# The S5 operator matrices moved from the middle of a diffusion layer to its beginning, beside the context's first feed-forward

## The chip, the cores and the metric

The kernel runs on one core of a Trainium2 chip, as one launch. The metric is the device time of that launch in microseconds, the median of three runs. The core has five engines with in-order queues: TensorE (PE: matmul, and PEld for its weight loads), VectorE (DVE), ScalarE (ACT), GpSimd (POOL) and SyncE (SP). In this kernel every DMA is issued from the SP queue, and a DMA that has to wait there holds back all that stand behind it.

## The reference, cut to what matters

```python
x   = half_ffn(x, mod_x, 0, ...)      # latents, 512 tokens, SwiGLU, width 1024, hidden 2816
ctx = half_ffn(ctx, mod_c, 0, ...)    # context, 256 tokens, same weights
hc  = modulate(ctx, norm_g[l, 1], mod_c[3], mod_c[4])
hx  = modulate(x, norm_g[l, 1], mod_x[3], mod_x[4])
out_c, ctx_states = token_mixers(hc, 1, zero_states(...), p, need_ctx)   # only the states are used
out_x, _ = token_mixers(hx, rows, ctx_states, p, True)
x = x + mod_x[5] * out_x
x = half_ffn(x, mod_x, 2, ...)
return rmsnorm(x, final_g)

def token_mixers(h, ...):             # S5 scan beside RWKV-7 scan, each in both directions
    proj = h @ w_in
    dt = exp(log_dt); mag = exp(dt * lam_re)
    ab = mag * (cos(dt * lam_im) + 1j * sin(dt * lam_im))
    z = (ab - 1) / lam; bb = z * b     # S5: 32 groups, 64 states, 16 channels each
    s5: s = ab * s + bb @ u; y = real(c @ s)
    rwkv: S = S * w + (S @ aa) bb^T + v k^T; y = S @ r      # 8 heads of 64
    ...
```

Neither the S5 matrices (powers of `ab`, `z`, and products of them with `b` and `c`) nor their inputs depend on the tokens: they can be made at any time before the first S5 scan.

## The kernel before, in words

The program is written by generators ("streams") that a planner class `Plan` runs in turn. Each stream has a priority number and yields what it needs next: a tile, an event by name, or a pair such as `("V", 600)`, which asks that the planned backlog of VectorE is at most 600 ns. `Plan.run` takes the stream with the lowest number whose needs are met at the planned time of TensorE, and the instructions are put into the engines' queues in that order. The planner's order is fixed when the program is built; on the chip only the queues and the semaphores count. A recording layer issues every instruction, so in the profile nearly all of them have the line L209, and tiles tell them apart.

**The dense work** is a stream of priority 9 (`dn`). It walks a list of weight tiles of 128 output columns: SP loads `raw` (512 KB), ACT casts it to the high half `wh`, DVE or POOL subtracts to make the low half `wl`, and PE takes three matmuls for each 128x128 tile (`hx,wh`, `hx,wl` and a second `wh` with the low half of the input; `ah`/`al` are the hidden activations in the down products). The list holds the context's first FFN (C, 256 columns, tiles `hc`, output `c`), the latents' first FFN (X, 512 columns, `hx`, output `x`), and from its eighth item on, among the latter, the context's input projections (`win`).

**The start.** `mods01` (priority 1) makes the first eight modulation pieces: two loads of `wmod` (512 KB each, four buffers), eight PE matmuls on each, an ACT copy to `mrow`, two PE matmuls `sel,mrow` into bank 6, and a DVE addition `mod<-b,bmod`. Bank 6 is a single buffer, so a `sel` matmul waits for the DVE addition before it. `norm0` sums the context's squares (`accc`), and after it the first FFN matmul (`hc,wh`) runs. `bg_a` makes the other modulations during the context's FFN and posts `wm`.

**`s5_build`** makes the S5 matrices. Its prelude is 85 small DVE operations in three parts (two exponentials and the sine's argument, 38, and 6 behind the two ACT sines; the powers `pw` and the factor `z`, 35; their products `pz`, 6). Then 16 blocks follow, each of 6 POOL operations (four `ms`, two `X`), 4 DVE copies (`cb`), 4 PE transposes (`ident,X`), 4 PE matmuls (`cb,X`), two ACT copies (`gst`, `kst`) and 6 DMAs (`hb`, `hk` in, `GTd`, `Kd` out). A second stream `outputs` has 16 blocks of 4 DVE `mh`, 2 DVE `H`, and DMAs (`hc` in, `Hd` out). At the end `Kd` is read back and turned into `KTd` (15 DMAs) and `KTe` (8 DMAs), and the event `s5b` is posted.

**The context's mixer** is laid out by `ctx_run` (priority 3). After the context's norm it opens the pool of the S5 matrices, adds `s5_build`, and then the projections. The scan stage waits for `s5b` among others:

```python
yield ["s5b", "winc"] + [f"{n}c{j}" for n in ("pb", "vr") for j in range(4)]
```

That stage loads `AB`, `Z`, `AT` (the products of the RWKV part, stored before as `abk`, `vt`, `lf`), `U` and `gt` for S5, solves a triangular system on DVE (`prod<-Tl,AT` and `Tl<-Tl,prod`, 62 operations), sends the solution through DRAM (`ti`, `tt`, `T`), and then runs four chunks on PE (`T,M`, `tt,w`, `ident,AB`, `Z,M`, `R,tt`, ...). What is left of the latents' FFN (`X`, dense) fills gaps of this stage; its last part waits for an event posted after the scan. The latents' mixer later has the same steps.

Of the kernel before, what the change touches and what calls it, by code (L numbers as in the profile page):

```python
# [27 lines left out]
MFB = 2  # L28
SPD = 0
WOL = 4  # L30
S5V = 600
S5Q = 3000
MPV = 1200
SPLIT_AT = 0
S5P = 3
FILLP = 5
RECP = 0
GATE0 = 0
# [245 lines left out]
class Kern:  # L284
# [575 lines left out]
    def phase_a(self):  # L860
        nc, a, sch, X, C = self.nc, self.a, self.sch, self.X, self.C
        with ExitStack() as es:
            self.hid = {}
            self.wxs, self.wx = self.right("wx")
            self.w_slots(self.wx, 1, 0, self.n_gate)
            self.hcs, hcp = self.right("hcp")
            C.h = [hcp.tile([128, KT, NCT], F32R, name=f"hc{i}") for i in range(2)]
            wrs, self.wxr = self.right("wxr")
            self.w_slots(self.wxr, 0, 1)
            self.cas, C.fp = self.right("ca")  # L870
            C.fp2 = C.fp
            C.res = C.fp.tile([128, KT, NCT], F32, name="c1")
            C.acc = [[C.fp.tile([128, 256], F32, name=f"accc{i}") for i in range(2)]]
            sch.post("fp0c")
            wms, self.wm = self.right("wm")
            st = [sch.add(self.mods01(), 1), sch.add(self.norm0(C), 0)]
            sch.add(self.dn, 9)
            sch.run(*st)
            nxs, self.nx = self.right("nx")
            X.res = es.enter_context(self.pool("rp")).tile([128, KT, NX], F32, name="x1")  # L880
            sch.add(self.bg_a(wms, nxs), 4)
            sch.add(self.norm0(X), 5)
            self.ctxg = sch.add(self.ctx_run(es, wrs), 3)

            def body(b, c, k, pb):
                return self.modulated(X.fp2, X.res[:, k, c], pb, 1, k, 0, [t[:, k, c] for t in X.h])

            def last():
                yield ["rwc"]
                yield from self.norm(X.fp2, X, 0, body)  # L890

            sch.run(sch.add(last(), 1))
            sch.run(sch.add(self.w_retire(self.wy), 0))
            self.wys.close()
# [13 lines left out]
    def ctx_run(self, es, wrs):  # L908

        X, C, sch = self.X, self.C, self.sch  # L910
        yield ["wm", "dl0c0", "hx17"]
        X.fp = es.enter_context(self.pool("fpx"))
        sch.post("fp0x")
        self.dbanks = (0, 5, 2)

        def body(b, c, k, pb):
            return self.modulated(C.fp, C.res[:, k], pb, 1, k, 1, [t[:, k] for t in C.h])

        yield from self.norm(C.fp, C, 0, body)
        self.cas.close()  # L920
        yield from self.w_retire(self.wxr)
        wrs.close()
        self.sbs, sb = self.right("sb")
        sch.add(self.s5_build(sb), S5P)
        qs, C.q = self.right("qc")
        self.phase_b1(C)
        for p, g in self.b1_gens:
            sch.add(g(C), p)
        yield ["s5b", "winc"] + [f"{n}c{j}" for n in ("pb", "vr") for j in range(4)]
        qs.close()  # L930
        self.sbs.close()
        self.hcs.close()
        rws, C.rw = self.right("rwc")
        self.rw_setup(C.rw)
        s5s, C.sp = self.right("s5c")
        C.hs = C.sp.tile([128, 32, 2, 32], F32, name="hs")
        self.dbanks = (0, 5)
        for p, g in ((0, self.rw_main(C)), (1, self.rw_pre(C)), (1, self.rw_solve(0, C.rw)), (2, self.s5_rec(C)),
                     (3, self.s5_in(C))):
            sch.add(g, p)  # L940
        yield ["step3", "s5recc"]
        s5s.close()
        rws.close()
        self.wms, wm = self.right("wm2")
        self.fill = sch.add(self.fill_run(wm), FILLP)
        X.fp2 = es.enter_context(self.pool("fpx2"))
        X.acc = [[X.fp2.tile([128, 256], F32, name=f"accx{b}{i}") for i in range(2)] for b in range(2)]
        self.wys, self.wy = self.right("wy")
        self.w_slots(self.wy, 2, 0, self.n_win)
        self.dbanks = (0, 5, 1)  # L950
        sch.post("rwc")
        sch.post("fp0x2")


    def s5_build(self, sb):
# [109 lines left out]
        def outputs():  # L1065

            nxt = load(0, "hc", a["s5C"])
            for n, (d, h2) in enumerate(todo):
                (Ct, c), nxt = nxt, load(n + 1, "hc", a["s5C"]) if n < 15 else None
                yield [Ct, ("V", S5V)]  # L1070
                H, ms = half("H"), half("mh")
# [11 lines left out]
                                      H[:, r].rearrange("p (e f) -> p e f", e=2))  # L1083
            self.sch.post("s5h")

        self.sch.add(outputs(), S5P)
        nb, nx = load(0, "hb", a["s5B"]), load(0, "hk", a["s5C"])
        for n, (d, h2) in enumerate(todo):
            (B, c), (Ct, c) = nb, nx
            if n < 15:  # L1090
                nb, nx = load(n + 1, "hb", a["s5B"]), load(n + 1, "hk", a["s5C"])
            yield [B, ("P", S5Q)]
            ks = slice(7, None, -1) if d == 0 else slice(0, 8)
            X, ms = half("X"), half("ms")
            for o, (r0, b0, r1, b1, op) in enumerate(terms):
                Pg.tensor_mul(r4(ms[:, 0]), bk(pz, r0, ks, c), bb(B[:, b0]))
                Pg.tensor_mul(r4(ms[:, 1]), bk(pz, r1, ks, c), bb(B[:, b1]))
                Pg.tensor_tensor(X[:, o], ms[:, 0], ms[:, 1], op=op)
            yield [X, Ct, ("A", 1500)]
            for q in range(2):  # L1100
                p = slice(q * 64, (q + 1) * 64)
                V.tensor_copy(cb[p, 0, :, q * 16:(q + 1) * 16], Ct[p, 0])
                V.tensor_scalar(cb[p, 1, :, q * 16:(q + 1) * 16], Ct[p, 1], -1.0, None, op0=OP.mult)
            pb = self.bank(7)
            xe = lambda r, e: X[:, r, e * 128:(e + 1) * 128]
            for e in range(2):
                for r in range(2):
                    PE.transpose(pb[:, (2 * e + r) * 128:(2 * e + r + 1) * 128], xe(r, e), self.ident)
            st = sb.tile([128, 2, 256], F32, name="gst", bufs=1)
            A_.copy(st, pb.rearrange("p (e f) -> p e f", e=2))  # L1110
            nc.sync.dma_start(self.GTd[2 * h2:2 * h2 + 2, :, d].rearrange("e p f -> p e f"), st)
            yield [cb]
            pk = self.bank(6)
            for e in range(2):
                o = pk[:, e * 32:(e + 1) * 32]
                PE.matmul(o, xe(0, e), cb[:, 0, e], start=True, stop=False)
                PE.matmul(o, xe(1, e), cb[:, 1, e], start=False, stop=True)
            ks = sb.tile([128, 64], F32, name="kst")
            A_.copy(ks, pk[:, 0:64])
            nc.sync.dma_start(Kd[d, :, h2 * 64:(h2 + 1) * 64], ks)  # L1120
        yield ["s5h"]

# [1016 lines left out]
```

## Time and profile before

| | |
|---|---|
| three runs | 1898.08, 1900.58 and 1901.99 us, median 1900.58 |
| the profiled execution | 1891.72 us, span 1890.0 us, granted PE clock 0.939 of full |
| busy in the span | PE 1672.3 us (88%), DVE 996.4 (53%), ACT 716.9 (38%), POOL 687.5 (36%) |
| chain that ended last | PE 56%, DVE 14%, DMA 14%, ACT 6%, POOL 3%, SP queue 3% |

All views are of the profiled execution. Busy time is what an engine's instructions took; idle time of an engine that nothing waits for costs nothing. PE is the engine with the most work, so a stretch is read by how much of it PE was idle or had a clock below 1.00, and by what ended its idle time.

The stages by time: the modulations and loads to about 97 us, the context's FFN to 277.5, the context's projections among the latents' FFN to 690, the context's scan to 805.6, then the rest of the latents' FFN, the latents' mixer and the second FFN.

### The profile page before, as it was taken

The numbers are of one execution on the slowest core, as the hardware profiler recorded it, in microseconds if no ns is written. First come the engines' busy times: TensorE is split into PE (matmuls) and PEld (weight loads), VectorE is DVE, ScalarE is ACT, GpSimd is POOL, SyncE is SP. The second block draws the span as 40 slices with busy tenths as digits, with TensorE's granted clock in tenths as the row PEclk, the third lists the DMA queues.
The fourth block names the chain that finished last, engine by engine and source line by source line (L and its number), as shares of the span: only waits on it lengthen the run. The fifth ranks groups of instructions, "written<-read, shape, count | busy, mean of one in ns | idle before, by whom it ended". The sixth has DMA issues, their size and how long they took to land.

```text
span 1890.0 us, 33157 instructions
## 1 busy us (share of the span) xinstructions
PE 1672.3 (88%) x13208; PEld 1400.3 (74%) x13208; DVE 996.4 (53%) x1747; ACT 716.9 (38%) x1200; POOL 687.5 (36%) x815
## 2 busy tenths in 40 slices
PE   6889999999999988778976789968697999999996
PEld 3689987778878867665544567758587988888886
DVE  3376564755558728355788855643343433333335
ACT  3355442545463212535443333443443332222222
POOL 0144231555764314621334537660065421111111
PEclk9999999999999999888988889979799999999998
DMA  9955541335454474433753566466364223323231
GB/s 310 331 167 195 183 155 57 113 106 159 143 160 140 141 190 151 119 123 128 252 160 105 148 223 188 118 172 176 123 215 159 67 69 101 99 91 101 98 101 56
DMA packets 235626, 278.43 MB, mean 147 GB/s; under 512 B 93616, under 2 KB 186800, under 8 KB 234448
## 3 DMA queue, kind: packets, MB, share of 16 engines
q1 hardware_dynamic: 235472, 276.32, 47.8%
q8 instruction: 104, 1.70, 0.4%
q14 instruction: 50, 0.41, 0.1%
HBM read 234.31 MB, written 43.22 MB: 147 GB/s over the span
## 4 chain that ended last, share of the span: by engine, by line
PE 56%; DVE 14%; DMA 14%; ACT 6%; issue 4%; POOL 3%; SPq 3%; DVEq 0%; ACTq 0%; POOLq 0%
PE b L209 56%; DMA wmod<-in_wmod 3%; SPq L209 3%; POOL wl L209 2%; ACT wh L209 2%; DMA Hd<-H 2%; DMA raw<-in_wgu 2%; DVE st L209 1%; DVE mh L209 1%; DVE wl L209 1%; DMA gt<-gates 1%; DVE rs L209 1%; DVE prod L209 1%; DVE cvr L209 1%; DVE H L209 1%
## 5 line engine op out<-in xcount | busy, mean ns | idle before, releaser
L209 PE MATMUL b<-hx,wh 128*128 128x512 f32 (+1 forms) x2432 | 698.2, 374 | 22.6 <-ACT wh L209 10.9
L209 POOL TENSOR_TENSOR wl<-raw,wh 128x1024 fp32r<-128x1024 f32 x135 | 329.3, 2443 | 822.0 <-ACT wh L209 748.1
L209 PEld LDWEIGHTS b<-hx,wh 128*128 128x128 f32 x2432 | 439.1, 194 | 106.7 <-issue 19.0
L209 PE MATMUL b<-hx,wl 128*128 128x512 f32 (+1 forms) x1216 | 448.6, 369 | 7.6 <-POOL wl L209 6.0
L209 ACT CAST wh<-raw 128x1024 fp32r<-128x1024 f32 x273 | 283.1, 1046 | 196.3 <-DMA raw<-in_wgu 69.8
L209 DVE TENSOR_TENSOR wl<-raw,wh 128x1024 fp32r<-128x1024 f32 x138 | 187.3, 1358 | 276.9 <-ACT wh L209 274.5
L209 PEld LDWEIGHTS b<-hx,wl 128*128 128x128 f32 x1216 | 235.7, 194 | 47.9 <-POOL wl L209 8.6
L209 PE MATMUL b<-ah,wh 128*128 128x512 f32 (+1 forms) x560 | 196.8, 351 | 3.6 <-ACT wh L209 2.0
L209 PE MATMUL b<-ah,wl 128*128 128x512 f32 (+1 forms) x560 | 194.9, 348 | 1.9 <-POOL wl L209 1.9
L209 PE MATMUL b<-al,wh 128*128 128x512 f32 (+1 forms) x560 | 194.7, 348 | 0.0
L209 PE MATMUL b<-hc,wh 128*128 128x256 f32 x928 | 173.1, 287 | 1.2 <-ACT hc L209 1.2
L209 PEld LDWEIGHTS b<-hc,wh 128*128 128x128 f32 x928 | 145.8, 192 | 10.9 <-issue 8.2
L209 PE MATMUL b<-hc,wl 128*128 128x256 f32 x464 | 131.7, 284 | 0.0
L209 PEld LDWEIGHTS b<-ah,wh 128*128 128x128 f32 x560 | 108.0, 193 | 16.6 <-ACT wh L209 2.2
L209 PEld LDWEIGHTS b<-ah,wl 128*128 128x128 f32 x560 | 107.9, 193 | 15.2 <-POOL wl L209 2.1
L209 ACT CAST ah<-prod 128x512 fp32r<-128x512 f32 (+1 forms) x68 | 36.6, 538 | 212.6 <-DVE prod L209 212.5
L209 PEld LDWEIGHTS b<-al,wh 128*128 128x128 f32 x560 | 107.8, 192 | 12.1
L209 ACT ACTIVATE sil<-b 128x512 f32<-128x512 f32 (+1 forms) x68 | 35.0, 515 | 149.8 <-PE b L209 149.6
L209 PEld LDWEIGHTS b<-hc,wl 128*128 128x128 f32 x464 | 89.3, 192 | 0.0
L209 DVE TENSOR_TENSOR prod<-sil,b 128x512 f32<-128x512 f32 (+1 forms) x68 | 39.6, 582 | 93.0 <-PE b L209 74.4
L209 DVE SCALAR_TENSOR_TENSOR x1c<-b,gp,x1c 128x512 f32<-128x512 f32 (+1 forms) x67 | 43.9, 662 | 81.2 <-PE b L209 81.2
L209 PE MATMUL b<-wmod,zs 128*32 128x256 f32 x576 | 54.3, 465 | 19.3 <-DMA wmod<-in_wmod 19.1
(289 smaller groups left out, 2331.0 us busy)
## 6 DMA issues: line engine op xcount, KB each, us to landing
raw<-in_wgu SPq DMA_DIRECT2D x132, 512.0 KB, 3.9
wmod<-in_wmod SPq DMA_DIRECT2D x72, 512.0 KB, 5.3
raw<-in_wdn SPq DMA_DIRECT2D x66, 512.0 KB, 3.7
raw<-in_win SPq DMA_DIRECT2D x49, 512.0 KB, 4.0
gt<-GTd SPq DMA_DIRECT2D x32, 256.0 KB, 3.8
abk<-st SPq DMA_DIRECT2D x8, 1024.0 KB, 5.5
AB<-abk SPq DMA_DIRECT2D x8, 1024.0 KB, 6.3
GTd<-gst SPq DMA_DIRECT2D x16, 256.0 KB, 2.4
```

The lines of the kernel that those rows point to most:

```text
L209: r = f(out, *args, **kw)
```

## The change

The pool `sb` is opened in `phase_a`, under the buffers of the context's FFN, and the stream `s5_build` is added there, before the planner has run anything, with priority 6. The pool of the latents' FFN (`fpx`) is opened only after the context's norm is done and the context's FFN pool (`ca`) is closed. Inside `s5_build`, the 16 blocks and `outputs` wait for `wm`, the transposes use bank 4 in place of bank 7, the two DMAs out wait in the plan for their copies, and the allowed planned backlogs become 250 ns for DVE and 600 ns for POOL.

```diff
--- before.py
+++ after.py
@@ -28,11 +28,11 @@
 MFB = 2
 SPD = 0
 WOL = 4
-S5V = 600
-S5Q = 3000
+S5V = 250
+S5Q = 600
 MPV = 1200
 SPLIT_AT = 0
-S5P = 3
+S5P = 6
 FILLP = 5
 RECP = 0
 GATE0 = 0
@@ -865,6 +865,7 @@
             self.w_slots(self.wx, 1, 0, self.n_gate)
             self.hcs, hcp = self.right("hcp")
             C.h = [hcp.tile([128, KT, NCT], F32R, name=f"hc{i}") for i in range(2)]
+            self.sbs, sb = self.right("sb")
             wrs, self.wxr = self.right("wxr")
             self.w_slots(self.wxr, 0, 1)
             self.cas, C.fp = self.right("ca")
@@ -875,6 +876,7 @@
             wms, self.wm = self.right("wm")
             st = [sch.add(self.mods01(), 1), sch.add(self.norm0(C), 0)]
             sch.add(self.dn, 9)
+            sch.add(self.s5_build(sb), S5P)
             sch.run(*st)
             nxs, self.nx = self.right("nx")
             X.res = es.enter_context(self.pool("rp")).tile([128, KT, NX], F32, name="x1")
@@ -909,19 +911,17 @@
 
         X, C, sch = self.X, self.C, self.sch
         yield ["wm", "dl0c0", "hx17"]
+        self.dbanks = (0, 5, 2)
+
+        def body(b, c, k, pb):
+            return self.modulated(C.fp, C.res[:, k], pb, 1, k, 1, [t[:, k] for t in C.h])
+
+        yield from self.norm(C.fp, C, 0, body)
+        self.cas.close()
         X.fp = es.enter_context(self.pool("fpx"))
         sch.post("fp0x")
-        self.dbanks = (0, 5, 2)
-
-        def body(b, c, k, pb):
-            return self.modulated(C.fp, C.res[:, k], pb, 1, k, 1, [t[:, k] for t in C.h])
-
-        yield from self.norm(C.fp, C, 0, body)
-        self.cas.close()
         yield from self.w_retire(self.wxr)
         wrs.close()
-        self.sbs, sb = self.right("sb")
-        sch.add(self.s5_build(sb), S5P)
         qs, C.q = self.right("qc")
         self.phase_b1(C)
         for p, g in self.b1_gens:
@@ -1083,6 +1083,7 @@
                                       H[:, r].rearrange("p (e f) -> p e f", e=2))
             self.sch.post("s5h")
 
+        yield ["wm"]
         self.sch.add(outputs(), S5P)
         nb, nx = load(0, "hb", a["s5B"]), load(0, "hk", a["s5C"])
         for n, (d, h2) in enumerate(todo):
@@ -1101,13 +1102,14 @@
                 p = slice(q * 64, (q + 1) * 64)
                 V.tensor_copy(cb[p, 0, :, q * 16:(q + 1) * 16], Ct[p, 0])
                 V.tensor_scalar(cb[p, 1, :, q * 16:(q + 1) * 16], Ct[p, 1], -1.0, None, op0=OP.mult)
-            pb = self.bank(7)
+            pb = self.bank(4)
             xe = lambda r, e: X[:, r, e * 128:(e + 1) * 128]
             for e in range(2):
                 for r in range(2):
                     PE.transpose(pb[:, (2 * e + r) * 128:(2 * e + r + 1) * 128], xe(r, e), self.ident)
             st = sb.tile([128, 2, 256], F32, name="gst", bufs=1)
             A_.copy(st, pb.rearrange("p (e f) -> p e f", e=2))
+            yield [st]
             nc.sync.dma_start(self.GTd[2 * h2:2 * h2 + 2, :, d].rearrange("e p f -> p e f"), st)
             yield [cb]
             pk = self.bank(6)
@@ -1117,6 +1119,7 @@
                 PE.matmul(o, xe(1, e), cb[:, 1, e], start=False, stop=True)
             ks = sb.tile([128, 64], F32, name="kst")
             A_.copy(ks, pk[:, 0:64])
+            yield [ks]
             nc.sync.dma_start(Kd[d, :, h2 * 64:(h2 + 1) * 64], ks)
         yield ["s5h"]
```

How this moves instructions is seen on three engines. The first place is the start of the program on VectorE: `mod`, `A` and `accc` belong to the modulations and the context's norm, `th` to `z` to the prelude of `s5_build`. Before, from the first `mod` on:

```order
L209 TENSOR_TENSOR mod<-b_168,bmod 128x4
L209 SCALAR_TENSOR_TENSOR A<-mod,ng 128x2 x2
L209 TENSOR_TENSOR mod<-b_190,bmod 128x4
L209 TENSOR_TENSOR mod<-b_209,bmod 128x4
L209 SCALAR_TENSOR_TENSOR A<-mod,ng 128x2 x2
L209 TENSOR_TENSOR accc<-accc,sq 128x256 x7
L209 TENSOR_TENSOR mod<-b_253,bmod 128x4
```

With the change, the rows from the end of the prelude's first part on; ahead of them stand the first `mod`, its two `A`, and 37 operations of that part:

```order
L209 TENSOR_SCALAR th<-th 128x32
L209 TENSOR_TENSOR cs<-cs 128x32
L209 TENSOR_SCALAR cs<-cs 128x32
L209 MEMSET pw 128x32 x2
L209 TENSOR_TENSOR pw<-mag,cs 128x32
L209 TENSOR_TENSOR pw<-mag,sn 128x32
L209 TENSOR_TENSOR mod<-b_254,bmod 128x4
L209 TENSOR_TENSOR ms<-pw 128x32 x4
L209 TENSOR_TENSOR pw<-ms 128x32 x2
L209 TENSOR_TENSOR ms<-pw 128x64 x4
L209 TENSOR_TENSOR pw<-ms 128x2x32 x2
L209 TENSOR_TENSOR ms<-pw 128x128 x4
```

The 44 operations of the first part (the 6 behind the sines among them) now stand between the first and the second `mod`, the 35 of the second part between the second and the third, and the last 6 behind the seven `accc`, ahead of the fourth `mod`. On ACT the two sines stand ahead of the third `mrow`.

The second place is GpSimd in the first half of the context's FFN; `wl` is the low half of a weight, `hx` the latents' normalised input, `ms` and `X` are S5 blocks. Before:

```order
L209 TENSOR_TENSOR hx_110<-mh,hx_109 128x256 x2
L209 TENSOR_TENSOR wl<-raw,wh 128x1024 x2
L209 TENSOR_TENSOR hx_110<-mh,hx_109 128x256 x2
L209 TENSOR_TENSOR wl<-raw,wh 128x1024 x2
L209 TENSOR_TENSOR hx_110<-mh,hx_109 128x256 x2
L209 TENSOR_TENSOR wl<-raw,wh 128x1024 x2
L209 TENSOR_TENSOR hx_110<-mh,hx_109 128x256
L209 TENSOR_TENSOR wl<-raw,wh 128x1024
L209 TENSOR_TENSOR hx_110<-mh,hx_109 128x256
L209 TENSOR_TENSOR wl<-raw,wh 128x1024 x13
L209 TENSOR_TENSOR accc_133<-accc_133,sq 128x256 x3
```

With the change:

```order
L209 TENSOR_TENSOR hx_110<-mh,hx_109 128x256 x2
L209 TENSOR_TENSOR wl<-raw,wh 128x1024
L209 TENSOR_TENSOR ms<-pz,hb 128x256 x2
L209 TENSOR_TENSOR X<-ms 128x256
L209 TENSOR_TENSOR ms<-pz,hb 128x256 x2
L209 TENSOR_TENSOR X<-ms 128x256
L209 TENSOR_TENSOR wl<-raw,wh 128x1024
L209 TENSOR_TENSOR hx_110<-mh,hx_109 128x256 x2
L209 TENSOR_TENSOR ms<-pz,hb 128x256 x2
L209 TENSOR_TENSOR X<-ms 128x256
L209 TENSOR_TENSOR ms<-pz,hb 128x256 x2
L209 TENSOR_TENSOR X<-ms 128x256
```

A block of S5 (four `ms`, two `X`) stands between one `wl` and the next where nothing stood before. Up to the context's norm there are 31 `wl` (26 before), 40 `ms` and 20 `X` (none before) on GpSimd, and on VectorE 33 `wl` (38 before), 24 `mh`, 12 `H` and 40 `cb` (none before). The other 6 of 16 blocks follow by the start of the latents' FFN.

The third place is TensorE at the context's scan: `T,M` is the first product with the solution, `tt,w`, `ident,AB` and `Z,M` follow from it, `hx,wh` and `hx,wl` are dense matmuls of the latents' FFN. Before:

```order
L209 MATMUL b_7790<-AB 128x64
L209 MATMUL b_7791<-AB 128x64
L209 MATMUL b_7790<-AB 128x64
L209 MATMUL b_7791<-AB 128x64
L209 MATMUL b_7832<-T_7758,M 32x32 x16
L209 MATMUL b_7866<-tt_7148,w 32x32 x16
L209 MATMUL b_7888<-ident,AB 128x128 x4
L209 MATMUL b_7894<-ident,AB 128x128 x4
L209 MATMUL b_7908<-Z_7160,M 64x64 x16
L209 MATMUL b_7935<-AB 128x64
```

With the change:

```order
L209 MATMUL b_7116<-hx_110,wh 128x512
L209 MATMUL b_7116<-hx_109,wl 128x512
L209 MATMUL b_7129<-T_7036,M 32x32 x16
L209 MATMUL b_7116<-hx_109,wh 128x512
L209 MATMUL b_7116<-hx_110,wh 128x512
L209 MATMUL b_7116<-hx_109,wl 128x512
L209 MATMUL b_7116<-hx_109,wh 128x512
L209 MATMUL b_7116<-hx_110,wh 128x512
L209 MATMUL b_7116<-hx_109,wl 128x512
L209 MATMUL b_7157<-tt_6540,w 32x32 x16
L209 MATMUL b_7179<-ident,AB 128x128 x4
L209 MATMUL b_7185<-ident,AB 128x128 x4
```

Before, `T,M` stood behind the last dense matmul of that stretch, and none stood between the steps of a chunk; now three to nine dense matmuls stand between them. From the last `st` product of the context's projections to the first `T,M` PE now has 156 dense 512-wide matmuls, 16 groups of 16 `U,gt` and two groups of `AB` grams, and some 420 dense 512-wide matmuls are left behind the chunks. On SP, the eight `KTe` now stand well ahead of the last `abk` and `lf` stores, and the loads of `AB`, `Z` and `AT` follow directly on these.

## Rows read from the trace of the kernel before

**Rows 1.** Windows: stretch, length, busy us per engine (instructions), PE clock, DMA share, GB/s.

```profile
0.00:97.00 97.00, 74.56 (x596) 48.44 (x596) 35.07 (x89) 32.90 (x66) 11.82 (x19) 0.98 0.96 320
109.00:277.50 168.50, 164.52 (x1365) 163.49 (x1365) 108.58 (x158) 83.14 (x124) 66.44 (x34) 0.98 0.57 183
277.50:690.00 412.50, 395.15 (x2234) 329.21 (x2235) 254.17 (x475) 170.58 (x278) 198.40 (x192) 0.97 0.44 127
600.00:650.00 50.00, 50.00 (x219) 40.74 (x217) 39.80 (x53) 12.58 (x15) 20.64 (x9) 1.00 0.48 136
690.00:752.80 62.80, 52.51 (x429) 41.05 (x427) 39.11 (x68) 15.68 (x44) 20.21 (x22) 0.92 0.64 192
752.80:765.50 12.70, 4.72 (x65) 4.16 (x64) 4.54 (x13) 2.32 (x3) 11.22 (x39) 0.68 0.38 119
765.50:805.60 40.10, 32.63 (x736) 28.76 (x736) 15.72 (x28) 24.51 (x48) 25.11 (x76) 0.93 0.44 102
```

**Rows 2.** Timeline of the SP queue: start, length, instruction, count.

```profile
100.61 8.74 SPq L209 DMA_DIRECT2D raw<-in_wgu  x2
...
589.94 0.38 SPq L209 DMA_DIRECT2D abk<-st  x1
...
655.00 7.27 SPq L209 DMA_DIRECT2D Hd<-H  x4
...
685.58 6.17 SPq L209 DMA_DIRECT2D KTe<-KTd  x8
```

**Rows 3.** Timeline of TensorE around the context's scan, idle before in brackets.

```profile
704.90 1.07 PE L209 MATMUL b<-U,gt 128*64 128x32 f32 x16 [7.52 <-DMA U<-udc]
...
752.46 0.39 PE L209 MATMUL b<-ah,wl 128*128 128x512 f32 x1
...
759.60 2.29 PE L209 MATMUL b<-AB 64*128 64x64 f32 x16 [5.71 <-DVE M L209]
...
764.00 1.06 PE L209 MATMUL b<-T,M 32*32 32x32 f32 x30 [1.10 <-DMA T<-ti]
```

**Rows 4.** Timeline of VectorE: first and last of the triangular solve's instructions.

```profile
711.16 0.18 DVE L209 TENSOR_TENSOR prod<-Tl,AT 128x31 f32<-128x31 f32 x1
...
755.67 0.36 DVE L209 TENSOR_TENSOR Tl<-Tl,prod 128x31 f32<-128x31 f32 x1
```

**Rows 5.** Timeline of TensorE, the same steps in the latents' mixer.

```profile
1096.83 1.08 PE L209 MATMUL b<-st 64*32 64x32 f32 x64 [0.69 <-ACT hs L209]
...
1168.05 0.24 PE L209 MATMUL b<-T,M 32*32 32x32 f32 x2 [2.45 <-DMA T<-ti]
```

**Rows 6.** Timeline of the program's start, VectorE and TensorE.

```profile
9.22 0.16 DVE L209 TENSOR_TENSOR mod<-b,bmod 128x4 f32<-128x4 f32 x1 [5.64 <-PE b L209]
...
25.49 1.01 PE L209 MATMUL b<-sel,mrow 128*128 128x2 f32 x4 [0.55 <-ACT mrow L209]
...
39.74 1.10 PE L209 MATMUL b<-hc,wh 128*128 128x256 f32 x2 [1.18 <-ACT hc L209]
```

**Rows 7.** Windows over the S5 prelude of 85 small VectorE operations.

```profile
319.69:331.10 11.41, 11.41 (x63) 9.88 (x62) 9.80 (x46) 1.45 (x5) 2.39 (x1) 1.00 0.14 46
336.60:348.30 11.70, 11.70 (x54) 9.45 (x53) 11.42 (x43) 5.62 (x6) 5.33 (x4) 0.96 0.50 126
```

**Rows 8.** Timeline at 320 us, GpSimd and VectorE side by side.

```profile
320.09 2.39 POOL L209 TENSOR_TENSOR wl<-raw,wh 128x1024 fp32r<-128x1024 f32 x1 [8.06 <-ACT wh L209]
320.12 2.39 DVE L209 TENSOR_SCALAR nn<-nn 128x32 f32<-128x32 f32 x1
```

**Rows 9.** One tile's instructions: count, min/median/max ns, first and last start.

```profile
L209 DVE TENSOR_TENSOR wl<-raw,wh x35: 1207/1226/2396, 107.8 to 272.1; 128x1024 fp32r<-128x1024 f32 x35
L209 POOL TENSOR_TENSOR wl<-raw,wh x23: 2395/2406/2845, 111.9 to 272.7; 128x1024 fp32r<-128x1024 f32 x23
...
L209 POOL TENSOR_TENSOR ms<-pz,hb x64: 637/658/1636, 347.9 to 541.0; 128x256 f32<-128x256 f32 x64
L209 POOL TENSOR_TENSOR X<-ms x32: 726/742/1599, 349.6 to 541.7; 128x256 f32<-128x256 f32 x32
```

More of the change, by code (lines that the diff above doesn't have):

```diff
@@ L911, in ctx_run @@
         yield ["wm", "dl0c0", "hx17"]
-        X.fp = es.enter_context(self.pool("fpx"))
-        sch.post("fp0x")
         self.dbanks = (0, 5, 2)
@@ L920, in ctx_run @@
         self.cas.close()
+        X.fp = es.enter_context(self.pool("fpx"))
+        sch.post("fp0x")
         yield from self.w_retire(self.wxr)
         wrs.close()
-        self.sbs, sb = self.right("sb")
-        sch.add(self.s5_build(sb), S5P)
         qs, C.q = self.right("qc")
```

## The prediction

> **What bounds the kernel now.** I read the busy times by stage first, then the timelines of the queues at the places that the change touches. The windows [rows 1] show that TensorE is the engine that the others serve. Up to 97 us it is busy for 74.56 us only, with a DMA share of 0.96: here the loads set the time. In the context's FFN (109 to 277.5) it idles for 4.0 us of 168.5. In the projections (277.5 to 690) it idles for 17.4 of 412.5. The costly place is the context's scan. From 690 to 752.8 it idles 10.3 us, and what it does runs at a granted clock of 0.92, so 52.51 x 0.08 = 4.2 us more go there. From 752.8 to 765.5 it idles 8.0 and has a clock of 0.68 (between its levels of 2.4 and 1.2 GHz), 4.72 x 0.32 = 1.5 us. From 765.5 to 805.6 it idles 7.5 and loses 2.3 by the clock. Together 33.8 us are lost in the scan.
>
> The SP timeline says why it comes so late [rows 2]. The context's last products are stored at 589.94, but four `Hd` stores of S5 leave at 655.00, and the last `KTe` copies at 685.58, taking 6.17. The scan's loads stand behind them. In TensorE's timeline [rows 3] the first `U,gt` waits 7.52 us for `U`, the last dense matmul of the stretch is at 752.46, and then the engine waits 5.71 us for `M` and once more at `T,M`, at 764.00. The reader is to see that the filler has run out there: the solve on VectorE, from 711.16 to 756.03, is 44.9 us long [rows 4], and nothing is left to hide its end.
>
> **The change part by part.** All sums are against the profiled 1891.72 us. The median of the runs shown lies 8.9 us above it, and I carry the difference to the median.
>
> *The start.* The 44 operations of the prelude's first part now stand between the first two modulation additions, 35 between the second and the third, and 6 ahead of the fourth. At 320 us the first part took 11.41 us and the other two 11.70 [rows 7]. One operation of 0.2 us took 2.39 there [rows 8], and in the second window two more were held by as much; no `wl` runs on GpSimd at the start, so I take 9.2 for the first part, 5 for the second and 2.1 for the third. The first addition stands at 9.22 [rows 6] and the inputs are there about 1 us later, so the second addition comes at about 19.7 and the third at 24.9. Behind it stand seven `accc` (about 3.6) and the 6 operations, so the fourth comes at 31. Bank 6 is single: each pair of `sel` matmuls waits for the addition before it, and TensorE's queue, with the next `wmod` products, waits with it. On ACT the third `mrow` stands behind the sines, hidden under the same wait. The fifth `sel` moves from 25.49 [rows 6] to about 31.3, 5.8 us, and the first FFN matmul from 39.74 to about 45.5. The four `wmod` buffers stay held for that time, so the SP queue cannot go on, and in a stretch bound by the loads this isn't won back.
>
> In the order TensorE has done 42 fewer context matmuls when the latents' norm is spread, at 164.52/1365 = 0.12 us [rows 1] another 5.0 us of work later on; one or two weights fewer are loaded in that stretch, at 512 KB and 320 GB/s 1.6 to 3.2 us of load that is moved out of it. Sum: **+8**. Bounds: +3, if the buffers that are full already hide half, and +13, if the fifth to eighth pieces each come late again. The twelve small loads of S5's first blocks are put where the SP queue waits 8.74 us anyway [rows 2]; at the 0.77 us of a `KTe` copy they need 9.3 at most, so I take 0.
>
> *The context's FFN.* Ten of 16 blocks on GpSimd and six of 16 `outputs` on VectorE move into it. GpSimd gets 40 x 0.66 + 20 x 0.74 = 41 us and 5 more `wl` of 2.41 us, 12; VectorE loses 5 `wl` of 1.23, 6, and gets 36 `mh` and `H`, priced between nothing and the 0.66 of an `ms` of their size, up to 24, say 15 [rows 9]. TensorE's own S5 work moves with them and costs the same wherever it runs. If the two engines were independent, GpSimd would have 66.4 + 53 = 119 busy us of 168.5 [rows 1] and nothing would wait. They are not: an operation of VectorE that started 0.03 us after a `wl` of GpSimd ended with it, after 2.39 us [rows 8]. Counted as one resource, the subtractions alone took 26 x 2.41 + 38 x 1.23 = 109 us before, and with the change 31 x 2.41 + 33 x 1.23 + 41 + 15 = 171 us, about as long as the stage. So some `wl` will come late for TensorE. I take **+4**, between 0 (the two still fit, since the first few `wl` fall into the load-bound stretch) and +12 (171 + 9 against 168.5). The context's pool `fpx` opens later, but the latents' first output is evacuated after the context's norm anyway: 0.
>
> The Trainium skill, page "SBUF — State Buffer", section "Who interferes with whom", says that a VectorE instruction with two SBUF inputs, or in a two-port mode, and a GpSimd instruction take a shared pair of ports exclusively, and that the loser waits for the whole instruction. By that rule the upper end, +12, would be the term and the total −2 us, 1899; the row of 2.39 us agrees with the rule as far as one row can.
>
> *The projections, 277.5 to 690.* They lose most of S5. Idle there is 17.4 of 412.5 us, 4.2%, against 2.4% in the stage before; at that share it would be 9.8, so −7.6. The rest of S5 still runs at its beginning: **−6**, between 0 and −9.
>
> *The scan.* `KTe` is out of the way and the context's products set the start. From the last `st` product to `T,M`, TensorE has 156 dense matmuls at 50.00/219 = 0.228 us [rows 1], 35.6 us, 16 groups of `U,gt`, 0.53 each at full clock (1.07 at half, [rows 3]), 8.5, and two groups of grams, about 2.2: 46 us. The chain itself (stores, loads, solve, three hops through DRAM) took 1168.05 − 1096.83 = 71.2 us in the latents' mixer [rows 5]. Its shortest form is the solve of 44.9, 8.0 from its end to `T,M` [rows 3, 4], and some 4 for the first hops, 57. I take 64, since here the loads stand directly behind the stores: TensorE will wait 18 us before `T,M` (11 to 25). The clock may fall for it. In the chunks 3 to 9 dense matmuls stand between steps, 0.7 to 2 us each, and should leave 4 of the 9.8 us lost there (0 to 10). 22 in place of 33.8: **−12**, between −23 and +1. What is late next is `T,M` itself, still behind VectorE's solve.
>
> The sum is +8 + 4 − 6 − 12 = **−6 us**: 1885.7 on the profiled execution, 1894.6 on the median.
>
> **The rivals.**
>
> *The shared port binds the context's FFN (slower).* One mechanism: GpSimd's 41 us of S5 and VectorE's subtractions exclude each other, so weights' low halves come late, and TensorE waits at `hc,wl` again and again. For it speaks the count of 171 us in 168.5; against it, that TensorE was 95.8% busy from 277.5 to 690 [rows 1] with these same blocks, though there a weight feeds twice as many columns. It decides from +14 on, where the sum passes 3.8: with 171 + 9 = 180 us of it against the 164.52 that TensorE works there [rows 1], +16: 8 − 6 − 12 + 16 = +6, about 1907. Chance 0.22.
>
> *The scan closes altogether (faster).* The chain has its shortest form, 57, and the chunks' gaps are filled: scan −21, and the start hides a part, +5: −18, 1883. For it speaks that no S5 load stands ahead of the scan; against it, the latents' 71.2 us. Chance 0.16.
>
> *The gain only changes its place (no difference).* The projections keep their idle time, if it comes from the projections' own hops between engines and not from S5 (0), and the chain takes 71, with 25 lost at `T,M`: scan −6. 8 + 4 − 0 − 6 = +6 at worst, +3 with half of the projections' part, 1904. Chance 0.16.
>
> **How the numbers follow.** A measurement of this kernel tells 0.2%, 3.8 us, from no change. The likeliest case has 0.46 and a range of its own of 1888 to 1900. About two thirds of it, and all of the closed scan, are faster by more than 0.2%: 0.30 + 0.16 = 0.46. Within 0.2% lie some of the likeliest, 0.14, and most of the third rival, 0.11: 0.25. Slower is the rest, 0.22 + 0.05 + 0.02 = 0.29. The range reaches from a closed scan that is not quite closed, 1880, to a port that binds, 1911.
>
> **What would show it.** The start: the second `mod` addition at about 20 us, the first `hc,wh` matmul at 45 to 49, holes in the DMA share between 12 and 35 us. The context's FFN: TensorE's waits for `wl` at 3 to 8 us against a few before; over 12 would be the port. The projections: idle time of about 11 us. The scan: `KTe` before the last `lf`, no 7.5 us wait for `U`, one wait of 11 to 25 us for `T` or `M`, dense matmuls between the chunks' steps. The prediction is wrong if the first FFN matmul has hardly moved, if GpSimd and VectorE overlap freely, if TensorE reaches `T,M` after the solution, or if the latents' FFN has too few matmuls left.

## The result, and the profile after

The changed kernel takes 1921.38 us in the median of its runs, the kernel before 1899.78 in runs beside it: ratio 1.0108, 95% interval 1.0075 to 1.0140. It is slower by 21.6 us, where I had forecast 6 us faster, and lies outside the range of 1880 to 1911.

The windows of the changed kernel, cut at the same points of the program as [rows 1]: the last modulations, the context's norm, its last `st` product, the last chunk of its scan, and the latents' norm, which comes at 876.0 us (853.4 before):

```profile
0.00:110.00 110.00, 78.10 (x580) 51.91 (x580) 50.54 (x188) 33.48 (x70) 11.97 (x20) 0.91 0.86 283
110.00:330.20 220.20, 198.19 (x1568) 194.09 (x1567) 155.60 (x237) 95.01 (x152) 139.86 (x106) 0.94 0.57 172
330.20:625.80 295.60, 277.13 (x1659) 231.71 (x1659) 162.19 (x286) 127.98 (x217) 107.16 (x101) 0.96 0.44 129
625.80:728.00 102.20, 94.67 (x1244) 74.66 (x1230) 58.33 (x109) 44.52 (x97) 56.89 (x139) 0.97 0.57 163
728.00:876.00 148.00, 135.88 (x718) 115.55 (x717) 59.28 (x107) 41.03 (x64) 24.94 (x19) 0.94 0.33 103
```

As in the prediction, a stage's loss is TensorE's idle time plus its busy time times what the granted clock lacks of 1.00. This table has both kernels, us:

| stage | before | after | predicted change | measured |
|---|---|---|---|---|
| start, to the last modulations | 28.0 | 38.9 | +8 | +10.9 |
| context's FFN | 7.3 | 33.9 | +4 | **+26.6** |
| projections | 29.2 | 29.6 | −6 | +0.4 |
| scan | 34.7 | 10.3 | −12 | **−24.4** |
| rest of the latents' FFN | 18.8 | 20.3 | 0 | +1.5 |

Together +15.0, against 22.6 between the two latents' norms; the clock in the rows has two digits, and 0.01 of some 780 busy us is 8 us, so the table is good for where, not for the last microseconds. (Cut into windows of 5 us, the same sum is +16.5, with +24.5 in the context's FFN; what is left of the 22.6 I did not follow.)

*The start* went as written. In the timeline of VectorE and TensorE the second, third and fourth `mod` additions stand at 19.67, 24.82 and 30.68 (19.7, 24.9 and 31 predicted), the fifth `sel` at 32.73 (31.3) and the first context matmul at 47.43 (45.5), against [rows 6]:

```profile
9.27 0.16 DVE L209 TENSOR_TENSOR mod<-b,bmod 128x4 f32<-128x4 f32 x1 [5.96 <-PE b L209]
...
19.67 0.15 DVE L209 TENSOR_TENSOR mod<-b,bmod 128x4 f32<-128x4 f32 x1
...
24.82 0.15 DVE L209 TENSOR_TENSOR mod<-b,bmod 128x4 f32<-128x4 f32 x1
...
30.68 0.16 DVE L209 TENSOR_TENSOR mod<-b,bmod 128x4 f32<-128x4 f32 x1
...
32.73 1.01 PE L209 MATMUL b<-sel,mrow 128*128 128x2 f32 x4 [0.54 <-ACT mrow L209]
...
47.43 1.10 PE L209 MATMUL b<-hc,wh 128*128 128x256 f32 x2 [1.18 <-ACT hc L209]
```

*The scan* gained twice what I had put down. `KTe` leaves at 514.18 (685.58 before, [rows 2]), and TensorE reaches `T,M` at 686.05 without a wait; from the last `st` product at 625.8 it took 60 us (64 predicted), and TensorE had 54 us of work in them (46 predicted). Timelines of SP and TensorE:

```profile
514.18 5.99 SPq L209 DMA_DIRECT2D KTe<-KTd  x8
```

```profile
686.05 0.69 PE L209 MATMUL b<-T,M 32*32 32x32 f32 x32
```

*The context's FFN* is where the time went. VectorE's timeline there shows an output block meeting the one ahead of it:

```profile
232.64 2.52 DVE L209 SCALAR_TENSOR_TENSOR H<-mh 128x256 f32<-128x256 f32 x1
235.20 0.76 DVE L209 TENSOR_TENSOR mh<-pw,hc 128x256 f32<-128x256 f32 x2
239.71 0.43 DVE L209 TENSOR_TENSOR H<-mh 128x256 f32<-128x256 f32 x1 [3.75 <-DMA Hd<-H]
240.05 0.41 DVE L209 TENSOR_TENSOR prod<-sil,b 128x256 f32<-128x256 f32 x1
...
247.28 5.08 DVE L209 TENSOR_TENSOR mh<-pw,hc 128x256 f32<-128x256 f32 x2
```

The rows of SP, GpSimd and TensorE (in this order) at the same place:

```profile
235.10 0.94 SPq L209 DMA_DIRECT2D Hd<-H  x2
```

```profile
247.16 4.92 POOL L209 TENSOR_TENSOR wl<-raw,wh 128x1024 fp32r<-128x1024 f32 x2 [2.87 <-ACT wh L209]
```

```profile
241.90 0.39 PE L209 MATMUL b<-ah,wh 128*128 128x256 f32 x1 [2.41 <-ACT wh L209]
...
253.69 0.47 PE L209 MATMUL b<-hc,wh 128*128 128x256 f32 x2 [2.27 <-DVE c L209]
```

`H` has one buffer. Its stores leave at 235.10, and the next block's first `H` has to wait until they have landed: VectorE stands for 3.75 us. Behind it in its queue are `prod`, `al` and a `wl`. ACT's next `wh` stands behind `ah`, which needs that `prod`, and TensorE stands for 2.41 us until 241.90. At 247.28 two `mh` take 5.08 us, while two `wl` run on GpSimd; at 235.20, with GpSimd idle, a pair took 0.76. `c` comes late, and TensorE waits 2.27 us for it. The view of VectorE's waits sums up those of `H` for 119 to 329 us (us in all, times, longest):

```profile
DVE H L209 <- DMA Hd<-H: 13.9, 4, 4.6
```

What VectorE did for S5 from 110 to 330.2 us is listed by groups (busy us and mean ns behind the bar):

```profile
L209 DVE TENSOR_TENSOR mh<-pw,hc 128x256 f32<-128x256 f32 x24 | 22.9, 995 | 0.1
L209 DVE SCALAR_TENSOR_TENSOR H<-mh 128x256 f32<-128x256 f32 x6 | 9.1, 1524 | 0.2
L209 DVE COPY cb<-hk 64x32 f32<-64x32 f32 x20 | 8.7, 437 | 0.1
L209 DVE TENSOR_TENSOR H<-mh 128x256 f32<-128x256 f32 x6 | 4.5, 750 | 14.0 <-DMA Hd<-H 13.9
L209 DVE TENSOR_SCALAR cb<-hk 64x32 f32<-64x32 f32 x20 | 4.0, 199 | 0.0
```

The 36 `mh` and `H` took 36.5 us, the 40 `cb` 12.7. TensorE's longest wait of the stage in all is for `c`; for weights' low halves it hardly waits longer than before. First two of its waits with the change, then those for `wl` before:

```profile
PE b L209 <- DVE c L209: 6.2, 3, 2.8
PE b L209 <- POOL wl L209: 3.8, 3, 1.9
```

```profile
PE b L209 <- POOL wl L209: 3.1, 2, 1.9
PE b L209 <- DVE wl L209: 0.7, 1, 0.7
```

### The profile page after: what moved, and what is told of

It reads as the page before. It is cut to its first block, busy times and chain, and to the rows that moved or that the text cites. A ratio compares the mean times of both kernels' runs of the same rounds, so it can differ in the third digit from the quotient of the medians.

```text
span 1919.5 us, 33103 instructions
## 1 busy us (share of the span) xinstructions
PE 1693.3 (88%) x13208; PEld 1414.7 (74%) x13208; DVE 983.0 (51%) x1753; ACT 707.4 (37%) x1193; POOL 685.2 (36%) x809
## 4 chain that ended last, share of the span: by engine, by line
PE 53%; DMA 9%; DVE 7%; ACT 4%; issue 3%; POOL 2%; SPq 1%; DVEq 0%; ACTq 0%; POOLq 0%
PE b L209 53%; POOL wl L209 1%; DMA gt<-gates 1%; DMA raw<-in_win 1%; ACT wh L209 1%; DMA Hd<-H 1%; DMA gt<-GTd 1%; SPq L209 1%; DMA wmod<-in_wmod 1%; DVE st L209 1%; DVE cvr L209 1%; DVE rs L209 1%; DMA yi<-yd 1%; DVE cvk L209 1%; POOL t L209 1%
## 5 line engine op out<-in xcount | busy, mean ns | idle before, releaser
L209 PE MATMUL b<-hx,wh 128*128 128x512 f32 (+1 forms) x2432 | 703.0, 376 | 18.2 <-ACT wh L209 10.4
L209 POOL TENSOR_TENSOR wl<-raw,wh 128x1024 fp32r<-128x1024 f32 x129 | 314.6, 2442 | 844.2 <-ACT wh L209 736.6
L209 DVE TENSOR_TENSOR wl<-raw,wh 128x1024 fp32r<-128x1024 f32 x144 | 197.2, 1370 | 273.6 <-ACT wh L209 271.2
L209 PE MATMUL b<-hc,wh 128*128 128x256 f32 x928 | 178.7, 293 | 4.6 <-DVE c L209 3.4
L209 PEld LDWEIGHTS b<-hc,wh 128*128 128x128 f32 x928 | 150.0, 197 | 14.8 <-issue 10.2
L209 PEld LDWEIGHTS b<-al,wh 128*128 128x128 f32 x560 | 109.1, 195 | 12.4 <-DVE al L209 0.2
L209 ACT CAST ah<-prod 128x512 fp32r<-128x512 f32 (+1 forms) x68 | 36.6, 538 | 219.1 <-DVE prod L209 219.1
L209 ACT ACTIVATE sil<-b 128x512 f32<-128x512 f32 (+1 forms) x68 | 35.1, 515 | 164.7 <-PE b L209 164.5
L209 PE MATMUL b<-wmod,zs 128*32 128x256 f32 x576 | 57.5, 497 | 20.3 <-DMA wmod<-in_wmod 20.2
```

The costliest lines, as they stand in the source:

```text
L209: r = f(out, *args, **kw)
```

## The experiments

Each experiment edits the changed kernel, if not said otherwise. Ratios are to the kernel before, run in turn with it on the same chip, with 95% intervals. The three columns of loss, from each one's own profile, are cut as in the table above.

| run | ratio | start | context's FFN | scan |
|---|---|---|---|---|
| before | 1 | 28.0 | 7.3 | 34.7 |
| changed | 1.0108 (1.0075-1.0140) | 38.9 | 33.9 | 10.3 |
| e12 changed, again | 1.0105 (1.0067-1.0143) | 38.6 | 34.5 | 11.4 |
| e1 prelude late | 1.0156 (1.0119-1.0193) | 33.7 | 39.5 | 11.0 |
| e2 outputs late | 1.0004 (0.9977-1.0030) | 37.8 | 19.7 | 10.4 |
| e3 store first | 1.0059 (1.0033-1.0085) | 38.6 | 22.2 | 13.9 |
| e4 = e1 + e2 | 1.0072 (1.0043-1.0102) | 31.6 | 29.5 | 7.7 |
| e5 = e2, prelude spread | 0.9981 (0.9956-1.0006) | 25.9 | 17.1 | 14.0 |
| e6 blocks and outputs late | 0.9960 (0.9934-0.9986) | 37.2 | 7.2 | 17.2 |
| e7 all of it late | 0.9975 (0.9943-1.0007) | 22.0 | 11.0 | 25.8 |
| e8 prelude spread | 1.0107 (1.0061-1.0152) | 26.6 | 36.6 | 15.1 |
| e9 before, with two yields | 1.0023 (1.0001-1.0045) | 22.6 | 8.0 | 22.3 |
| e10 = e6, prelude spread | **0.9935** (0.9912-0.9959) | 28.2 | 9.7 | 19.4 |
| e11 outputs alone early | 1.0189 (1.0154-1.0223) | 35.7 | 33.4 | 16.4 |
| e13 = e11, two `H`, one `X` | 1.0027 (1.0008-1.0047) | 37.9 | 19.5 | 15.3 |
| e14 = e10, two `H`, one `X` | 0.9985 (0.9963-1.0006) | 25.9 | 8.3 | 20.0 |

The planner answers every edit with an order that differs in later stages too, so a part of one run's ratio is not its edit's (some 1% between e11 and e13, below); what I call shown rests on the stage and the ratio together.

**e1 to e4: the prelude or the outputs later.** The edits:

```diff
         lre, lim, dt = C("lre"), C("lim"), C("ldt")
+        yield ["gp0"]                       # e1, e4
...
+            yield ["fp0x"]                  # e2, e4
             nxt = load(0, "hc", a["s5C"])
...
-                yield [Ct, ("V", S5V)]      # e3
+                yield [Ct, ("V", S5V)] + [self.Hd] * (n > 0)
```

> The changed kernel, but the S5 prelude (its loads and 85 VectorE operations) waits for the event gp0, behind the first eight modulations. Theory A (front and stores): the prelude holds the modulations, their loads and all behind them, about 10 us in the load-bound start. Then the first context matmul is back at 40 us and the time falls by 8 to 12 us, to 1909-1913. Rival B (shared port alone): the start's delay is made up in the load-bound stretch, and the kernel gains under 4 us, 1917 or more.

> The changed kernel, but the 16 output blocks (mh, H on VectorE and the Hd stores) wait until the context's norm is done. Theory A: in the context's FFN VectorE stands 13.9 us at H until its only buffer is stored, and evacuations, casts and low halves stand behind it; the stage (119 to 329 us) gets 11 to 16 us shorter and the time is 1905-1910. Rival B: what costs is GpSimd's S5 blocks against VectorE's subtractions; they stay, so 1917 or more. Both: KTe has some 100 us of slack, so the scan stays where it is.

> The changed kernel, but an output block is not put in before the stores of the block ahead are planned to have landed, so that VectorE finds its buffer H free. Theory A: the waits of H for Hd in the context's FFN fall from 13.9 us to under 5, and the time by 6 to 12 us, 1909-1915. Rival B: no change beyond 3 us, 1918-1924.

> Both edits at once: the prelude behind the first modulations and the output blocks behind the context's norm. Theory A: the two gains add, 20 to 27 us off the changed kernel: 1894-1901, about the kernel before or a little under it, with the scan as filled as in the changed kernel (T,M behind dense matmuls, under 12 us lost there). Rival B: under 8 us gained, 1913 or more.

e2 and e3 came out as theory A said, e2 beyond it: 1.04% (20 us) under the changed kernel, e3 0.5%. e1 and e4 refute it for the prelude: e1 is no faster than the changed kernel, and e4 is slower than e2. The first context matmul of e1 is at 40.10, as expected, and the start's loss falls by 5.2 us, but the next stage loses 5.6 us more, with 15 blocks in it in place of eleven. The windows of e1 show that the prelude costs time in its new place too (columns as in [rows 1]):

```profile
60.00:70.00 10.00, 7.70 (x74) 6.19 (x73) 4.25 (x6) 4.25 (x8) 2.39 (x1) 1.00 0.96 322
70.00:80.00 10.00, 7.54 (x65) 6.73 (x64) 7.96 (x44) 0.61 (x3) 0.00 (x0) 1.00 0.92 329
80.00:90.00 10.00, 7.62 (x55) 6.65 (x57) 7.31 (x18) 4.82 (x9) 4.77 (x2) 0.66 0.42 131
```

In one piece the prelude fills VectorE from 71 to 80 us (7.96 of 10) here. A `prod` stands behind it, which ACT's next `ah` and `wh` need; ACT is idle for 9.76 us, no weight is cast between 69.4 and 80.9, and from 80 to 90 us the DMA share falls to 0.42 and the clock to 0.66.

**e5 to e8: the prelude spread, and what stays behind the norm.** e5 and e8 put a `yield [("V", 0)]` behind each VectorE operation of the prelude. e6 and e7 move the gate:

```diff
-        yield ["wm"]
+        yield ["fp0x"]                      # e6: blocks and outputs
         self.sch.add(outputs(), S5P)
...
         lre, lim, dt = C("lre"), C("lim"), C("ldt")
+        yield ["fp0x"]                      # e7, this line alone: the prelude too
```

> Output blocks behind the context's norm as in e2, and the prelude put in one VectorE operation at a time wherever the plan has VectorE free, so that the first modulations stand ahead of it. e1 and e4 showed that a later prelude in one piece gains nothing, so two readings are left. Theory A: in one piece it holds VectorE for 9 and 5 us wherever it stands; spread, it holds nothing, the first context matmul is back at 40 us and the time is 5 to 10 us under e2 (ratio to before 0.995 to 0.998). Rival B: what is held at the start is made up by 110 us, and the ratio stays at 1.000 or above.

> The changed kernel with the prelude at the start, but all 16 S5 blocks and the output blocks behind the context's norm. Theory A: the context's FFN loses its S5 and its idle time (22 us from 119 us on) falls under 8 us; KTe stands behind the last lf store again, so the scan waits for it and its loss returns to 25-35 us; ratio 1.000 to 1.008. If the blocks on GpSimd had cost nothing there, as e2 suggests in part, the context's FFN gains under 5 us against e2.

> The whole of s5_build behind the context's norm: the old place with the new numbers, the new bank and the latents' pool opened late. It tells the place from the numbers. Theory A (the place decides): as the kernel before, ratio 0.997 to 1.003. Rival B (the numbers, or the late pool, have a price or a gain of their own): outside of it.

> The changed kernel with the prelude spread as in e5, output blocks where the change puts them. Theory A: 5 to 10 us under the changed kernel, ratio to before 1.005 to 1.008. Rival B: as the changed kernel, 1.010 or more.

Spread, the prelude costs the start nothing: its loss is 26 to 27 us, as before the change. In e8 most of that is given back: the context's FFN, with 15 blocks in it in place of eleven, loses 2.7 us more than in the changed kernel, the scan 4.8, and the ratio doesn't move; why the scan does, the runs leave open. e6 shows the other half. With no S5 block in it the context's FFN loses 7.2 us, as before the change, and the scan, against what I expected, keeps most of its gain, 17.2 us lost:

```profile
111.00:289.70 178.70, 174.99 (x1450) 173.99 (x1450) 111.41 (x168) 88.66 (x133) 69.65 (x35) 0.98 0.58 180
289.70:606.40 316.70, 301.88 (x1821) 252.95 (x1821) 209.40 (x349) 138.85 (x241) 169.29 (x167) 0.96 0.45 130
606.40:767.00 160.60, 147.82 (x1484) 119.83 (x1471) 81.34 (x138) 57.83 (x112) 74.25 (x150) 0.97 0.58 160
```

e7 against e6 shows what the early prelude is worth: it costs 11.4 us in the start and the context's FFN together, and gives back 8.6 in the scan, where `KTe` leaves at 639 us in place of 663, and 5.6 in the projections (26.9 lost against 32.5); the ratios are the same within their intervals. With all of S5 at its old place, e7 still loses 8.9 us less in the scan than the kernel before, so that part of the scan's gain is not the place's.

**e9 to e12.** e9 is the kernel before with the two `yield` lines ahead of the stores alone. e10 is e6 with the prelude of e5. e11 leaves the outputs where the change puts them and moves the blocks:

```diff
         yield ["wm"]
         self.sch.add(outputs(), S5P)
+        yield ["fp0x"]                      # e11
```

> The kernel before with one part of the change alone: the two stores of a block (GTd, Kd) are put into the SP queue only when their copies on ACT are planned to be done. In the built order this brings T,M to row 3494 on TensorE (3659 before) and KTe ahead. Theory C: part of the scan's gain that I put down to the place of S5 comes from these two lines; KTe leaves before 650 us (685.6 before), the loss in the scan falls by 8 to 20 us, ratio 0.990 to 0.997. Rival: the place alone does it, ratio 0.998 to 1.002 and KTe at 675 or later.

> As e6 (blocks and outputs behind the context's norm), with the prelude spread over free VectorE time at the start as in e5 and e8. Theory A: the loss up to about 100 us falls from 38 to 27 us as in e5 and e8, the context's FFN stays under 8 us, and the ratio is 0.989 to 0.994, the fastest of all. Rival B: what is gained at the start is given back by 330 us as in e8, ratio 0.995 to 0.998 as e6.

> The changed kernel with the 16 blocks on GpSimd behind the context's norm, and only the output blocks (VectorE, Hd stores) beside the context's FFN: the counterpart of e2. Theory A (VectorE held at H by its own store): 10 us or more over e6, ratio 1.001 to 1.008, with H's waits for Hd of 10 us or more in that stage. Rival B (only both together collide, on the shared port): as e6, ratio 0.994 to 0.999.

> The changed kernel once more, on the chip of these runs, so that the others are compared with it on one chip: ratio 1.008 to 1.014 as measured at first.

e9 refutes theory C for the time: the scan's loss falls by 12 us and `KTe` leaves at 659.7, but the projections lose 46.7 us (29.2 before), and the kernel is not faster. e12 repeats the first result. e11 is slower than either of its theories had it. In it the outputs alone cost as much in the context's FFN as outputs and blocks together in the changed kernel, but not the same number of them: the planner puts ten output blocks into the stage there and six here. By the counts of `X` and `H` in the stage (two for a block each; e13 follows below):

| run | S5 blocks in the stage | output blocks in it | its loss |
|---|---|---|---|
| e6 neither | 0 | 0 | 7.2 |
| e2 blocks alone | 16 | 0 | 19.7 |
| e11 outputs alone | 0 | 10 | 33.4 |
| e13 the same, two `H` | 0 | 10 | 19.5 |
| e3 both, no wait for the store | 14 | 4 | 22.2 |
| changed, both | 11 | 6 | 33.9 |

An estimate from these rows, if the loss grows evenly with the count: a block costs 12.5/16 = 0.8 us, an output block 26.2/10 = 2.6, and 1.2 with two `H`. The changed kernel then has 9 us from eleven blocks and 16 from six output blocks, nearly all of its 26.7 over e6; for e3 the same numbers give 16, and it has 15.0. The windows of e2 and e11, and e11's waits of VectorE and TensorE:

```profile
112.00:325.00 213.00, 197.18 (x1621) 193.84 (x1620) 137.57 (x228) 98.85 (x162) 149.26 (x128) 0.98 0.59 178
```

```profile
107.00:313.30 206.30, 182.02 (x1450) 178.42 (x1449) 152.67 (x214) 88.22 (x133) 105.01 (x49) 0.95 0.56 169
```

```profile
DVE H L209 <- DMA Hd<-H: 19.6, 7, 4.3
```

```profile
PE b L209 <- DVE c L209: 14.6, 5, 4.0
```

e2's waits of TensorE are of another kind. It waits for the tiles of S5's own blocks, whose transposes and matmuls stand in its queue, and only 0.9 us for a `wl`:

```profile
PE b L209 <- DVE cb L209: 7.2, 4, 2.1
PE b L209 <- POOL X L209: 4.1, 5, 1.7
PE b L209 <- ACT gst L209: 3.4, 1, 3.4
```

**e13 and e14: two buffers of H.**

```diff
-        half = lambda n: sb.tile([128, 2, 256], F32, name=n, bufs=1 + (n == "X"))
+        half = lambda n: sb.tile([128, 2, 256], F32, name=n, bufs=1 + (n == "H"))
```

> As e11 (output blocks beside the context's FFN, the other blocks behind its norm), with two buffers of H in place of one, and one of X in place of two to make room. Theory A (the store): H's waits for Hd in the stage from 107 us to the context's norm fall from 19.9 us to under 4, the stage's loss from 31 us to 12-20, and the ratio from 1.019 to 1.000-1.010. Rival B (VectorE's own time and the shared port): the waits fall, the loss does not, ratio 1.015 or more.

> As e10, the fastest so far, with two buffers of H and one of X. There H's 35.8 us of waits stand in the projections, where TensorE has more dense work to go on with. Theory A: the waits go, KTe leaves some 10 us earlier and the scan's loss falls a little: ratio 0.989 to 0.993. Rival B: the waits were hidden there, and one X holds GpSimd at its transposes: 0.993 to 0.998.

For the outputs alone, the wait for the store is shown to be the larger half: with two buffers no `H` waits for `Hd` any more, and the stage's loss falls from 33.4 to 19.5 us. The kernel gets 1.6% (31 us) faster, but not by that alone: the projections lose 21.6 us in place of e11's 40.9, though e11 has only 7.7 us of these waits there; why, the runs leave open. The changed kernel itself was not run with two `H`; e3, which takes its waits away in the plan, is the nearest. The stage's window, and the two largest waits of VectorE that are left:

```profile
107.00:298.10 191.10, 178.81 (x1450) 177.17 (x1450) 150.82 (x220) 88.82 (x134) 98.12 (x46) 0.96 0.61 184
```

```profile
DVE wl L209 <- ACT wh L209: 12.3, 11, 2.8
DVE prod L209 <- PE b L209: 10.1, 5, 3.4
```

What stays, 12.3 us above e6, I put down to VectorE's own time there and to its port, which these runs don't part: TensorE still waits 8.2 us for `c`, and 35 `wl` run on GpSimd (24 in e6). e14 is slower than e10 and came out nearest to rival B: its `KTe` leaves 26 us earlier, at 604.5, and the scan loses no less. Where the waits have room, a second `H` is worth nothing; that one `X` less costs is not shown by itself, but GpSimd waits 10.3 us for it in the projections, and not at all in e10.

**The version that beats both** is e10: 0.9935, 12 us under the kernel before and 33 under the changed one. Against e6, with its prelude in one piece, the intervals overlap, so the spreading's own gain is not shown: the start loses 9.0 us less, the context's FFN and the scan 4.7 more. Its windows, and the fifth `sel` and first context matmul on TensorE, at their places of before:

```profile
0.00:99.00 99.00, 77.83 (x579) 51.13 (x580) 51.02 (x189) 34.92 (x73) 10.37 (x20) 0.91 0.94 311
99.00:280.20 181.20, 174.97 (x1449) 173.52 (x1448) 110.34 (x167) 86.67 (x129) 62.10 (x32) 0.98 0.57 179
280.20:595.50 315.30, 300.94 (x1830) 253.46 (x1830) 188.72 (x347) 141.58 (x243) 164.62 (x167) 0.97 0.47 132
595.50:753.00 157.50, 143.89 (x1470) 117.03 (x1456) 85.98 (x141) 57.47 (x112) 72.36 (x149) 0.96 0.58 160
753.00:836.80 83.80, 72.32 (x445) 64.05 (x444) 39.15 (x84) 26.18 (x46) 17.51 (x14) 0.90 0.33 107
```

```profile
25.71 1.02 PE L209 MATMUL b<-sel,mrow 128*128 128x2 f32 x4 [0.55 <-ACT mrow L209]
...
39.94 1.10 PE L209 MATMUL b<-hc,wh 128*128 128x256 f32 x2 [1.19 <-ACT hc L209]
```

## Why the prediction was wrong, point by point

**The start, +8: right.** Mechanism and size held, +10.9. That it "isn't won back" was only half right: e6 and e7 show that an early prelude is paid back in the projections and the scan.

**The context's FFN, +4: the step that failed**, with +26.6 measured, above the bound of +12. I priced the moved `mh` and `H` at 15 us, and put two things at nothing: the 40 `cb` copies on VectorE, and the wait between the outputs, one buffer `H` that is filled again only when its store has landed. Measured are 36.5 us for `mh` and `H`, 12.7 for `cb` and 13.9 of waits, 63 us of VectorE's queue in place of 15. The wait was in the trace of before, 17.4 us in 10 waits between 277.5 and 690 us, in a stage where each weight feeds 512 columns; that such waits cost little there is borne out by e10 and e14: with 35.1 us of them in the projections and with none, these lose 23.4 and 28.4 us there. I had taken the rule "idle time of VectorE costs nothing" along into a stage where a weight lasts half as long, and TensorE had 4.0 us of idle time in 168.5. By the estimate from the table of counts, the wait is 8 of the 26.6 us (six times the 1.4 that a second `H` saves per output block in e13) or 12 (by e3, with its counts set off), the outputs' own time 7 and the blocks 9. In the changed kernel itself no run parts them.

**The rival with the shared port** had the right sign, but +16 and 1907 were too small as well, and its mechanism isn't what the rows show. It had weights' low halves come late and TensorE wait at them; TensorE's waits for `wl` are 4.2 us, against 3.8 before. What ran long beside GpSimd's operations, as at 232.64 and 247.28, was VectorE's S5: 36 `mh` and `H` at the 0.43 us of the row at 239.71 would be 15 us, as priced, and they took 36.5. TensorE then waited for `c`. And the sum that I gave for the page's rule was wrong: with +12 in place of +4 it is +2 us, 1903, not −2 and 1899.

**The projections, −6: wrong**, +0.4. They got rid of eleven of the 16 blocks and only six of the 16 output blocks, and idled as long as before (18.5 us, 17.4 before), as the third rival had it. In e6 and e10, where S5 is back in them, they lose 23 to 27 us, less than the 29.6 of the changed kernel. So S5 was not what they waited for.

**The scan, −12: right in kind, too small.** The stage came out as the rival that closes it, which I gave 0.16: −24.4. The chain was 60 us and not 64, and TensorE's work in it 54 us and not 46; both ends of my difference erred in the same direction. And the place beside the context's FFN was not needed for most of it: e6 has 17.5 of the 24.4 us, e7, with S5 at its old place, 8.9.

**The sum.** −6 + 2.9 + 22.6 + 6.4 − 12.4 + 1.5 = +15: the term of the context's FFN alone turns the sign.

## What to carry to other kernels

When work is moved beside another stage, list not only what its instructions take but every wait between them, a buffer that its own store must free above all, and ask what stands behind that wait in the in-order queue at the new place; a wait that was free beside wide matmuls can cost most of its length beside narrow ones (13.9 us for 19.6 of waits in e11). A block of small operations that nothing waits for is put in one at a time, and not as a lump, into a queue that feeds the loads' consumers. And move the parts one by one, and count how much of each lands in the stage: here 16 blocks alone cost 12.5 us in it, ten output blocks alone 26.2, and the prelude, spread, nothing at the start.

## What the runs showed of the hardware that I had not expected

A small store that frees a buffer is not cheap to wait for: from the issue of the two `Hd` stores at 235.10 to the next write of `H` at 239.71 it was 4.6 us, more than ten times what the write itself takes (0.43). The Trainium skill, page "SBUF — State Buffer", section "Who interferes with whom", says that the shared ports are held for a whole instruction; the two `mh` at 247.28 that took 5.08 us, under two `wl` on GpSimd of 4.92 us together, agree with it. And a lower clock stood behind such waits: TensorE waited 2.41 us before 241.90 and 1.94 before 244.34, and from 244.3 to 247.3 it ran at a granted 0.50, the lower of its two levels. The stretch from 110 to 330 us had 0.94 where the stage had 0.98 before, so that some 12 of its 33.9 lost us (3 of 7.3 before) are not idle time at all.
